# First mixer of a two-block model in an order that the kernel lays down itself, with fixed tile places, and the key search's row scale moved from VectorE to ScalarE

## The chip, the core and the metric

The kernel is one program on one core of a Trainium2 chip. The metric is device microseconds of one execution, from start to end; a run is compared by the median of its executions. The engines that matter here are TensorE (PE, matmuls), VectorE (DVE), ScalarE (ACT), GpSimd (POOL) and the DMA queue that SyncE (SP) issues. Each engine takes its instructions in the order in which they stand in its own queue; semaphores order the engines among each other.

## The reference, cut to what matters

The input is 512 tokens of 1024 values. The change lies in the first mixer and in the first step of the layer behind it:

```
h  = rmsnorm(x);  p = h @ w_in                    # 1024 -> 20 column blocks of 128
p_rw = p + mu0*(prev-p) + mu1*(next-p)             # token shift, first 16 blocks
r,k,v,wd,ad,gd = split(p_rw);  g = sigmoid(gd) @ g_up
for d in (forward, backward):                      # 8 heads of 64
    decay = exp(-exp(-softplus(-(w0+tanh(wd)@w_up))-0.5)); a = sigmoid(a0+ad@a_up)
    o += wkv7_scan(r, decay, k*(1+(a-1)*k_a), v, kk, a, reverse = d)   # delta-rule state, 64x64 a head
    bonus += sum(r*kd*r_k)*v
y_rwkv = (groupnorm(o) + bonus) * g;  y_pool = multiscale_pool(p[:, last 512])
x1 = x + concat(y_rwkv, y_pool) @ w_out
# next layer
h2 = rmsnorm(x1);  q = h2 @ wq                     # 16 column blocks f of 128
s  = q_f . keys_f   (128 scores a token and f);  top_k(s, 16)
```

Everything is float32. Behind the key search come routing, two passes over a 16,384 row expert table, and a second block; none of that is rewritten.

## The kernel before, in words

Data lie transposed: 128 features on the partitions, 512 tokens along the row. A matmul against a large weight is done in three passes in fp32r, with both operands split in a high and a low part (`Lin.mm`, L141; `Lin.mm_rows`, L154, which takes two column blocks at a time): `lo*whi`, `hi*wlo`, `hi*whi`. A weight block comes in by DMA (`wraw`), ACT copies its high part (L70, `whi`), DVE or POOL subtracts for the low part (L71, `wlo`). Blocks of w_in are loaded in four parts of two k steps, and a block is asked for one ahead (`lin.load(order[n + 1])` in `w_in`).

The first mixer runs from 0 to about 478 us. It computes w_in's 20 column blocks f (480 matmuls) and, in four quarters i of two heads, these steps: `front(i)` (L347; head norm L330 and L343, decay and gate projections L371, sigmoids, a scan, exponentials, then the in-chunk products `kb,za` and `rd,kb` L318), `invert(i)` (L435; inverts 32x32 triangles: a chain of small DVE operations L469/L470, transposes L473/L475, 32x32 matmuls L488 to L517), `solve(i)` (L523), `chain(i)` (L565; seven steps of the state over chunks, PE to DVE L585 and back) and `back(i)` (L589; group norm, bonus, gate). Gate (L231) and pooling (L257) lie in between. Then `project` multiplies with w_out in three pieces: `project(4, 4)` for the pooled half, `project(0, 3)` for quarters 0 to 2 and `project(3, 1)` for quarter 3; each of its blocks f ends with DVE adding the PSUM bank to `xt` (L655), and in the last piece also with the split `hu`, `lu` for the next layer (L77, L78) and the sum of squares `sums` (L86, L87). `inv_rms` and `spread` (L102, L108) turn that into `rb2`, the root of each token, along the row on all partitions.

The first `w_in` blocks, `front(0)` to `chain(0)`, the other `w_in` blocks with `back(0)`, and quarters 1 to 3 are written out in this order (L612 to L683). Which instruction stands where in each engine's queue is decided by the framework's scheduler, which may hoist over that order. Tiles come from rotating pools, two banks of PSUM each for `ppb`, `ppf` and `ppw`, one each for `ppi` and `ppz`.

The key search (L786 to L824) takes f = 0 and 1 by `mm_rows` and the other 14 by `mm`; each PSUM block goes through DVE (`q = ps * rb2`, L814), four matmuls with the keys (L817), one ACT copy of 128x512 (L820) and `top16` on DVE for four groups of tokens (L779 to L784). For f under 8, `normed(f)` makes `h` on DVE (L797), and PE turns a part of it (L800).

Of the kernel before, what the change touches and what calls it, by code (L numbers as in the profile page):

```python
# [46 lines left out]

@with_exitstack
def tile_two_blocks(ctx: ExitStack, tc: tile.TileContext, a: dict, out: bass.AP):
    nc = tc.nc  # L50
    V, S, G, PE = nc.vector, nc.scalar, nc.gpsimd, nc.tensor
# [4 lines left out]

    const = mk(ctx, "const", 1)
    ident = const.tile([128, 128], F32, name="ident")
    vec = const.tile([128, NVEC], F32, name="vec")
    nc.sync.dma_start(vec, a["vec"])  # L60
# [12 lines left out]
    nb = mk(ctx, "nb", 2)  # L73
# [40 lines left out]
    class Lin:  # L114
# [47 lines left out]
    cx1 = ctx.enter_context(ExitStack())  # L162
    with ExitStack() as c1:
        pooled_d = dram.tile([4, 128, T], F32, name="pooled_d")
        gate_d = dram.tile([4, 128, T], F32, name="gate_d")
        ppb = mk(c1, "ppb", 2, PSUM)
        ppf = mk(c1, "ppf", 2, PSUM)
        ppi = mk(c1, "ppi", 1, PSUM)
        ppz = mk(c1, "ppz", 1, PSUM)
        ppw = mk(c1, "ppw", 2, PSUM)  # L170
        lw = mk(c1, "lw", 1)
# [93 lines left out]
        def w_in(n):  # L265
# [6 lines left out]
            if 1 <= n and n + 1 < len(order):  # L272
                lin.load(order[n + 1])
# [1207 lines left out]
```

## Time and profile before

| | us |
|---|---|
| median of 3 runs (lowest to highest) | 2991.76 (2989.59 to 2994.38) |
| profiled execution | 2990.21 |
| its span | 2988.4 |
| PE busy in the span | 2858.1 (96%) |
| DVE busy | 1895.3 (63%) |
| ACT busy | 1198.6 (40%) |
| POOL busy | 937.7 (31%) |

PE is busy nearly all the time, but busy is not the same as quick: the profile also gives the clock that was granted to PE, as a share of full speed, and it falls in the first mixer. For a stretch of the span, idle time plus (1 - granted clock) times busy time is what PE lost against running through at full clock.

### The profile page before, as it was taken

To read this page: it belongs to the slowest core of one execution; us is meant where nothing else is said; L and a number is where in the kernel's file an instruction comes from. 1 tells how busy PE (TensorE), PEld (TensorE's weight loads), DVE (VectorE), ACT (ScalarE), POOL (GpSimd) and SP (SyncE) were. 2 spreads that over 40 slices of the span, in tenths; PEclk is the share of its full clock that TensorE was granted. 3 is DMA by queue.
4 is the path that set the end of the run, shared out by engine and by line. 5 is a ranking of instruction groups with operands and counts; after the bars stand their busy time and mean duration, and the time that the engine had idled before them with its cause. 6 is when DMAs were issued, how large, how long until landed. Compare 5 with 4: busy or idle time off the path is not lost.

```text
span 2988.4 us, 45289 instructions
## 1 busy us (share of the span) xinstructions
PE 2858.1 (96%) x17713; PEld 2394.9 (80%) x17713; DVE 1895.3 (63%) x3317; ACT 1198.6 (40%) x2073; POOL 937.7 (31%) x595
## 2 busy tenths in 40 slices
PE   8997899999999999999999999999999999999998
PEld 6666777799999877799999977888876667888887
DVE  7567637899997477777777786332269644633311
ACT  6344334247778333333333334332234343433322
POOL 1012134212331212143434414444431333244443
PEclk9898989999999999999999999999999999999999
DMA  3141123267886899999999952233331122322332
GB/s 117 58 133 31 41 63 133 71 196 262 293 304 246 297 312 315 317 313 312 316 318 326 320 174 72 98 99 95 96 104 50 59 62 62 113 89 94 99 93 77
DMA packets 201749, 495.46 MB, mean 166 GB/s; under 512 B 17616, under 2 KB 95312, under 8 KB 199616
## 3 DMA queue, kind: packets, MB, share of 16 engines
q1 hardware_dynamic: 164672, 358.34, 36.5%
q0 software_dynamic: 36864, 134.23, 12.9%
q8 instruction: 139, 2.28, 0.3%
q14 instruction: 74, 0.61, 0.1%
HBM read 446.53 MB, written 45.22 MB: 165 GB/s over the span
## 4 chain that ended last, share of the span: by engine, by line
PE 62%; DVE 19%; issue 7%; ACT 4%; DMA 3%; POOL 2%; SPq 0%; ACTq 0%; DVEq 0%; POOLq 0%
PE ps L141 32%; PE pss L736 12%; PE pv L1053 8%; DVE vl L987 2%; ACT vh L981 2%; DVE row L761 2%; PE ps L318 2%; PE pg L925 2%; POOL wlo L71 2%; DMA gate<-gates_d 1%; DVE o L918 1%; DVE ul L71 1%; DVE st L992 1%; DVE acc L766 1%; PE ps L154 1%
## 5 line engine op out<-in xcount | busy, mean ns | idle before, releaser
L71 POOL TENSOR_TENSOR wlo<-wraw,whi 128x1024 fp32r<-128x1024 f32 (+4 forms) x232 | 504.3, 2177 | 760.9 <-ACT whi L70 758.7
L70 ACT ACTIVATE whi<-wraw 128x1024 fp32r<-128x1024 f32 (+4 forms) x320 | 262.0, 822 | 691.6 <-PE ps L141 439.9
L755 POOL DMA_INDIRECT row<-peer_u,idx x128 | 163.3, 1275 | 494.1 <-DVE row L761 359.0
L141 PE MATMUL ps<-lo,whi 128*128 128x512 f32 x1112 | 295.4, 397 | 1.5 <-DVE pad L218 1.4
L141 PE MATMUL ps<-hi,whi 128*128 128x512 f32 x1112 | 295.8, 395 | 0.0
L141 PE MATMUL ps<-hi,wlo 128*128 128x512 f32 x1112 | 294.2, 395 | 1.0 <-POOL wlo L71 0.8
L141 PEld LDWEIGHTS ps<-hi,wlo 128*128 128x128 f32 x1112 | 207.8, 189 | 50.9 <-issue 6.5
L141 PEld LDWEIGHTS ps<-lo,whi 128*128 128x128 f32 x1112 | 207.4, 189 | 51.4 <-issue 7.3
L755 POOL DMA_INDIRECT row<-peer_v,idx x128 | 168.9, 1320 | 253.7 <-DVE acc L766 216.8
L1053 PE MATMUL pv<-vl,gh 128*128 128x512 f32 x768 | 241.9, 396 | 6.9 <-DVE vl L987 3.9
L141 PEld LDWEIGHTS ps<-hi,whi 128*128 128x128 f32 x1112 | 207.6, 188 | 47.1 <-issue 5.1
L1053 PE MATMUL pv<-vh,gh 128*128 128x512 f32 x768 | 237.6, 391 | 0.0
L1053 PE MATMUL pv<-vh,gl 128*128 128x512 f32 x768 | 236.9, 390 | 0.0
L70 ACT ACTIVATE gh<-st 128x384 fp32r<-128x384 f32 x128 | 67.2, 525 | 409.7 <-DVE st L992 294.3
L736 PE MATMUL pss<-lo,uh 128*128 128x384 f32 x1024 | 207.8, 344 | 5.4 <-ACT st L740 5.4
L736 PE MATMUL pss<-hi,ul 128*128 128x384 f32 x1024 | 201.7, 337 | 4.0 <-DVE ul L71 4.0
L736 PE MATMUL pss<-hi,uh 128*128 128x384 f32 x1024 | 200.4, 336 | 0.0
L987 DVE TENSOR_TENSOR vl<-vraw,vh 128x1024 fp32r<-128x1024 f32 x128 | 161.4, 1261 | 49.9 <-ACT vh L981 48.8
L736 PEld LDWEIGHTS pss<-lo,uh 128*128 128x128 f32 x1024 | 181.2, 191 | 10.9 <-ACT st L740 6.1
L736 PEld LDWEIGHTS pss<-hi,ul 128*128 128x128 f32 x1024 | 180.8, 189 | 4.6 <-DVE ul L71 4.6
L1053 PEld LDWEIGHTS pv<-vl,gh 128*128 128x128 f32 x768 | 140.6, 188 | 52.1 <-DVE vl L987 25.2
L736 PEld LDWEIGHTS pss<-hi,uh 128*128 128x128 f32 x1024 | 180.5, 189 | 0.0
(439 smaller groups left out, 5209.6 us busy)
## 6 DMA issues: line engine op xcount, KB each, us to landing
uraw<-peer_ut SPq DMA_DIRECT2D x128, 512.0 KB
vraw<-peer_v SPq DMA_DIRECT2D x128, 512.0 KB
wraw<-ffn_w_in SPq DMA_DIRECT2D x88, 512.0 KB
gates_d<-stg SPq DMA_DIRECT2D x12, 2048.0 KB
gate<-gates_d SPq DMA_DIRECT2D x32, 768.0 KB
wraw<-w_in SPq DMA_DIRECT2D x40, 512.0 KB
wraw<-ffn_w_out SPq DMA_DIRECT2D x32, 512.0 KB
st_d<-st SPq DMA_DIRECT2D x58, 192.0 KB
```

Source lines behind the costliest of these rows:

```text
L70: S.activation(hi, src, AF.Copy)
L71: eng.tensor_sub(lo, src, hi)
L141: PE.matmul(ps, w_[:, k, :m], x_[:, k0 + k, :], start=n == 0, stop=n == last)
L154: PE.matmul(ps, w_[:, k, :], x_[:, k0 + k, :], start=k0 + k + n == 0, stop=k0 + k == self.kd - 1 and n == 2)
L318: PE.matmul(ps[j:j + 64], w_[j:j + 64], x_[j:j + 64], start=start, stop=stop, tile_position=(j, j))
L736: PE.matmul(ps, w_[:, k, :], x_[:, k, :ND], start=n == 0, stop=n == 23)
L755: G.indirect_dma_start(out=r, out_offset=None, in_=tab, in_offset=bass.IndirectOffsetOnAxis(ap=idx[:, i:i + 1], axis=0))
L761: V.scalar_tensor_tensor(r, r, 1.0, htok, op0=ALU.mult, op1=ALU.mult, accum_out=act[:, s:s + 1])
L925: PE.matmul(pg[:, i, :], oo[1][:, e + i, :], oo[0][:, e + i, :], start=True, stop=True)
L981: S.activation(vh, vld[b], AF.Copy)
L987: V.tensor_sub(vl, raw, vh)
L1053: PE.matmul(pv[t * 2 + e], l_[:, ts_], r_[:, e * 512:(e + 1) * 512], start=b == 0 and q == 0, stop=b == 127 and q == 2)
```

## The change

In the first mixer the engines are wrapped (`Engine`). While the plan is open, a call isn't issued; it is noted as a node with what it reads and writes (`Plan.note`; up to 1.4 us of like PE calls on one PSUM bank make one node). `Plan.flush` gives each node a rank, the longest estimated way to the end, and places the nodes by list scheduling: the engine that can start first takes, of its ready nodes, the one of highest rank. The nodes are then issued in the order of their planned starts, under `tc.manual_schedule()`, which leaves that order as it is. There are three flushes: behind w_in and quarter 0, behind `back(2)`, and at the mixer's end. `Turns` gives each tag fixed tiles taken in turn. A weight part is noted where it is used (`Lin.take`), and the plan decides how early it is loaded. In the second part `chain` and `back` write to `ppw` banks. All noted instructions carry the line of the issuing call, L222. The key search scales the scores by `rs2` in four ACT copies in place of scaling `q` on DVE.

```diff
+class Plan:
+    STEP, SLACK, UNIT = 0.05, 0.3, 1.4
...
+    def cost(self, e, op, args, kw):
+        size = max(_free(args[0]), _free(args[1]) if op in ("max", "tensor_reduce") else 0)
+        if e == "PE":
...
+            t = max((4 * n / 2400 if full else n / 2400) + 0.013 * (1 + full), 0.05)
+            t = t / 4 if k == 32 and m == 32 else t / 2 if m == 64 else t
+            return max(t, 0.014), t + 0.2, (k == 128, m >= 128, full)
...
+        for v in reversed(nodes):
+            v["rank"] = v["until"] + max((nodes[j]["rank"] for j in v["after"]), default=0.0) + self.STEP
...
+            i = max((i for i in waiting[e] if nodes[i]["ready"] <= t + self.SLACK),
+                    key=lambda i: (nodes[i]["rank"] - 2.0 * turn(nodes[i]) - 4.0 * max(0.0, nodes[i]["ready"] - t), -i))
...
+        order.sort(key=lambda i: nodes[i]["start"])
+        with self.tc.manual_schedule():
+            for i in order:
+                for real, op, args, kw in nodes[i]["calls"]:
+                    getattr(real, op)(*args, **kw)
...
+class Turns:
...
+        n = self.n[tag] = self.n.get(tag, -1) + 1
+        key = f"{tag}_{n % (bufs or self.bufs)}"
...
-    nb = mk(ctx, "nb", 2)
+    nb = turns(ctx, "nb", 3)
...
+        def take(self, f, p):
+            if (f, p) not in self.ready:
+                self.load_part(f, p)
+            return self.ready.pop((f, p))
...
-            if 1 <= n and n + 1 < len(order):
-                lin.load(order[n + 1])
...
-            po = qd["po"] = psb()
+            po = qd["po"] = psb(outs)
...
         for n in range(8, 20):
             w_in(n)
+        plan.flush()
         cw.close()
-        open_slots(1, "right")
-        open_slots(2, "right")
+        open_slots(1, "right", plan.free["PE"])
+        open_slots(2, "right", plan.free["PE"])
+        plan.begin()
+        outs = ppw
         front(1)
...
         back(2)
+        outs = ppb
+        plan.flush()
         slots[2][1].close()
         slots[1][1].close()
+        plan.begin()
...
-        rb2 = spread(psb(ppi), inv_rms(total(psb(ppi), sums), 1e-5), xu)
-        nc.sync.dma_start(x1_d, xt)
+        rs2 = inv_rms(total(psb(ppi), sums), 1e-5)
+        rb2 = spread(psb(ppi), rs2, xu)
+        SP.dma_start(x1_d, xt)
+        plan.flush()
...
-                    V.tensor_mul(q, ps, rb2)
+                    S.activation(q, ps, AF.Copy)
...
-                    S.activation(s_.rearrange("p t n -> p (t n)"), ps, AF.Copy)
+                    for t in range(4):
+                        S.activation(s_[:, t, :], ps[:, t * 128:(t + 1) * 128], AF.Copy, scale=rs2[:, t:t + 1])
```

Three places show how instructions move. The first is PE's queue where w_in ends and quarter 1 begins. Before, the last matmuls of w_in (L141) are followed at once by quarter 1's `kb,za`; all that quarter 1 needs ahead of it stands further up, among w_in. Then comes the head of quarter 2 (L330, L343, L371) and quarter 1's inversion (L488).

```order
L141 MATMUL ps<-lo,whi 128x512 x2
L141 MATMUL ps<-hi,wlo 128x512 x2
L141 MATMUL ps<-hi,whi 128x512 x2
L318 MATMUL ps<-kb,za 64x128 x16
L318 MATMUL ps<-cst,v 64x64 x16
L318 MATMUL ps<-cst,vf 64x64 x16
L318 MATMUL ps<-cst,za 64x64 x16
L318 MATMUL ps<-rd,kb 64x128 x32
```

The same place of the change; here `rd,th` belongs to `chain(0)`, `y,cst` and the first `cst,vf` to `back(0)`, `cst,e` and `ident,rsTrue` to quarter 1's head norm.

```order
L222 MATMUL ps_117<-rd_0_174,th_184 64x64 x2
L222 MATMUL ps_123<-lo_105,whi_128 128x512 x2
L222 MATMUL ps_123<-hi_104,wlo_129 128x512 x2
L222 MATMUL ps_123<-hi_104,whi_128 128x512 x2
L222 MATMUL ps_120<-y_197,cst_90 128x512
L222 MATMUL ps_156<-sg_159,rbo_153 128x512
L222 MATMUL ps_117<-cst_90,vf_186 128x2 x4
L222 MATMUL ps_158<-cst_90,e_0_154 128x2 x4
L222 MATMUL ps_158<-lora_91,wup_152 128x512
L222 MATMUL ps_120<-ident,rsFalse_198 64x128 x8
L222 MATMUL ps_156<-ident,rsTrue_1901 64x128 x8
L222 MATMUL ps_156<-lora_91,wup_152 128x512
```

Quarter 0 now lasts until w_in's last six matmuls, and quarter 1's head stands behind them; four more rows on (two `lora,wup` and the two transposes of v) comes its `kb,za`.

The second place is DVE's queue at the end of the mixer, `project(3, 1)`. Before:

```order
L78 SCALAR_TENSOR_TENSOR lu<-xt,vec,hu 128x512
L655 TENSOR_TENSOR xt<-xt,ps 128x512
L78 SCALAR_TENSOR_TENSOR lu<-xt,vec,hu 128x512
L87 TENSOR_TENSOR sums<-sums,sq 128x512
L78 SCALAR_TENSOR_TENSOR lu<-xt,vec,hu 128x512
L655 TENSOR_TENSOR xt<-xt,ps 128x512
L87 TENSOR_TENSOR sums<-sums,sq 128x512
L655 TENSOR_TENSOR xt<-xt,ps 128x512
```

and in the change, from the eighth and last addition to `xt` on:

```order
L222 TENSOR_TENSOR xt_3937<-xt_3937,ps_123 128x512
L222 TENSOR_TENSOR sums_3958<-sums_3958,pd_3943 128x512
L222 SCALAR_TENSOR_TENSOR lu_3957<-xt_3937,vec,hu_3956 128x512
L222 TENSOR_TENSOR sums_3958<-sums_3958,pd_3943 128x512
L222 SCALAR_TENSOR_TENSOR lu_3957<-xt_3937,vec,hu_3956 128x512
L222 TENSOR_SCALAR ms_3959<-ps_185 128x4
L222 SCALAR_TENSOR_TENSOR lu_3957<-xt_3937,vec,hu_3956 128x512
L222 RECIPROCAL rs_3960<-ms_3959 128x4
L222 SCALAR_TENSOR_TENSOR lu_3957<-xt_3937,vec,hu_3956 128x512 x5
L1018 SCALAR_TENSOR_TENSOR h<-xt_3937,vec,rb_3961 128x512 x4
L1000 MAX vals<-s 128x8 x2
```

All eight additions to `xt` and six of the seven sums now stand ahead of the first `lu`, and four `h` stand ahead of the first `top16`.

The third place is PE's queue there: before, `project(3, 1)` (L141) and the key search's `mm_rows` (L154) alternate,

```order
L154 MATMUL ps<-hu,wlo 128x512
L141 MATMUL ps<-pl,whi 128x512
L141 MATMUL ps<-ph,wlo 128x512
L141 MATMUL ps<-ph,whi 128x512
L154 MATMUL ps<-hu,whi 128x512
L154 MATMUL ps<-lu,whi 128x512
L154 MATMUL ps<-hu,wlo 128x512
L154 MATMUL ps<-hu,whi 128x512
```

and in the change `mm_rows` (L368) begins when `project(3, 1)` has ended:

```order
L222 MATMUL ps_123<-pl_3942,whi_3951 128x512
L222 MATMUL ps_123<-ph_3941,wlo_3952 128x512
L222 MATMUL ps_123<-ph_3941,whi_3951 128x512
L368 MATMUL ps<-lu_3957,whi 128x512
L222 MATMUL ps_185<-ones,sums_3958 128x1 x4
L368 MATMUL ps<-hu_3956,wlo 128x512
L368 MATMUL ps<-hu_3956,whi 128x512
L368 MATMUL ps<-lu_3957,whi 128x512
```

The sum of squares over the partitions (`ones,sums`) stands behind the first of the 48 `mm_rows` matmuls, where before it stood ahead of the last three.

## Rows read from the trace of the kernel before

**Rows 1.** Windows: length, busy us (PE, PEld, DVE, ACT, POOL), PEclk, DMA share, GB/s.

```profile
0.00:23.00 23.00, 15.32 (x57) 11.23 (x58) 14.39 (x35) 15.99 (x30) 2.93 (x10) 1.00 0.71 231
23.00:224.00 201.00, 182.24 (x1738) 136.42 (x1740) 129.63 (x238) 87.85 (x157) 19.41 (x23) 0.93 0.29 88
80.00:100.00 20.00, 16.78 (x279) 7.29 (x278) 14.31 (x38) 5.19 (x9) 1.18 (x2) 0.74 0.21 69
224.00:421.00 197.00, 167.61 (x3672) 141.87 (x3669) 123.95 (x242) 78.35 (x128) 37.64 (x38) 0.90 0.14 44
245.00:279.00 34.00, 24.20 (x609) 19.16 (x610) 26.38 (x54) 18.66 (x27) 8.62 (x9) 0.75 0.11 27
421.00:478.00 57.00, 52.14 (x219) 39.19 (x218) 25.77 (x38) 22.00 (x42) 28.71 (x26) 0.94 0.31 97
478.00:600.00 122.00, 109.37 (x537) 87.59 (x536) 104.22 (x531) 37.30 (x56) 42.23 (x21) 1.00 0.28 95
```

**Rows 2.** Waits of PE, 224 to 478: us, times, longest.

```profile
PE ps L488 <- DVE dt L473: 9.9, 3, 7.3
PE ps L141 <- POOL pl L71: 3.5, 3, 2.1
PE ps L318 <- DVE th L585: 1.9, 2, 1.2
```

**Rows 3.** Timeline of PE, quarter 0's head: start, busy us, instructions, [idle before].

```profile
41.86 0.95 PE L330 MATMUL ps<-cst,sq 128*128 128x2 f32 x8
...
58.99 1.96 PE L318 MATMUL ps<-kb,za 64*64 64x128 f32 x32 [1.46 <-DVE za L392]
```

**Rows 4.** Timeline of PE, quarter 2's head and quarter 1's inversion.

```profile
244.53 0.95 PE L330 MATMUL ps<-cst,sq 128*128 128x2 f32 x8
...
260.72 1.93 PE L488 MATMUL ps<-dt,lo 32*32 32x32 f32 x128 [7.33 <-DVE dt L473]
```

**Rows 5.** Timeline of PE, mixer's end and three steps of the key search.

```profile
465.11 0.39 PE L141 MATMUL ps<-pl,whi 128*128 128x512 f32 x1
...
484.83 1.13 PE L108 MATMUL ps<-ident,rs 128*128 128x128 f32 x8
...
539.37 1.13 PE L817 MATMUL ps<-keys,q 128*128 128x128 f32 x8 [0.52 <-DVE q L814]
540.34 0.27 PE L800 MATMUL pt<-ident,h 128*128 128x128 f32 x1
...
546.28 1.13 PE L817 MATMUL ps<-keys,q 128*128 128x128 f32 x8 [0.52 <-DVE q L814]
...
596.21 1.13 PE L817 MATMUL ps<-keys,q 128*128 128x128 f32 x8 [0.61 <-DVE q L814]
```

**Rows 6.** Timeline of DVE, first `top16` and the first instruction behind the last.

```profile
494.87 0.49 DVE L779 MAX8 vals<-s 128x8 f32<-128x128 f32 x2
...
603.13 0.29 DVE L833 CAST idf<-ids 128x256 f32<-128x256 uint32 x1
```

**Rows 7.** Groups of DVE, 462 to 495: busy us, mean ns, idle before.

```profile
L655 DVE TENSOR_TENSOR xt<-xt,ps 128x512 f32<-128x512 f32 x10 | 6.8, 681 | 4.3 <-PE ps L141 4.3
L78 DVE SCALAR_TENSOR_TENSOR lu<-xt,vec,hu 128x512 fp32r<-128x512 f32 x8 | 6.2, 775 | 1.1 <-ACT hu L77 1.1
L87 DVE TENSOR_TENSOR sums<-sums,sq 128x512 f32<-128x512 f32 x7 | 5.1, 732 | 0.0
```

**Rows 8.** Groups of all engines, 478 to 603.

```profile
L797 DVE SCALAR_TENSOR_TENSOR h<-xt,vec,rb 128x512 f32<-128x512 f32 x8 | 12.5, 1586 | 0.0
...
L814 DVE TENSOR_TENSOR q<-ps,rb 128x512 f32<-128x512 f32 x16 | 10.8, 678 | 3.5 <-ACT rb L111 1.9 <-PE ps L817 1.6
L820 ACT ACTIVATE s<-ps 128x512 f32<-128x512 f32 x16 | 9.5, 596 | 26.8 <-PE ps L817 25.8 <-DVE mr L782 1.0
...
L801 ACT ACTIVATE htok<-pt 128x128 f32<-128x128 f32 x8 | 2.2, 270 | 1.2 <-PE pt L800 1.2
```

**Rows 9.** Groups of ACT, 600 to 1000: a 128x128 copy with a pointer scale.

```profile
L921 ACT ACTIVATE o<-o,gtr 128x128 f32<-128x128 f32 x384 | 126.0, 393 | 42.4 <-DVE o L918 42.3
```

More of the change, by code (lines that the diff above doesn't have):

```diff
@@ new lines, in _free, with __init__, tile @@
+def _free(ap):
+    n = 1
+    for d in ap.shape[1:]:
+        n *= d
+    return n
+class Turns:
+    def __init__(self, plan, pool, bufs, born=0.0):
+        self.plan, self.pool, self.bufs, self.born, self.n, self.places = plan, pool, bufs, born, {}, {}
+    def tile(self, shape, dtype, tag=None, name=None, bufs=None):
+        tag, size = tag or name, 1
+        for d in shape[1:]:
+            size *= d
+        n = self.n[tag] = self.n.get(tag, -1) + 1
+        key = f"{tag}_{n % (bufs or self.bufs)}"
+        if key not in self.places:
+            t = self.places[key] = self.pool.tile([128, size], dtype, tag=key, name=key, bufs=1)
+            self.plan.born[t.tensor.name] = self.born
+        t = self.places[key][:shape[0], :size]
+        if len(shape) == 3:
+            t = t.rearrange("p (a b) -> p a b", b=shape[2])
+        elif len(shape) == 4:
+            t = t.rearrange("p (a b c) -> p a b c", b=shape[2], c=shape[3])
+        return t
@@ L55, in mk, with turns @@
         return c.enter_context(tc.tile_pool(name=name, bufs=bufs, side=side, reuse_waits="tile", **kw))
+    def turns(c, name, bufs, space=None, side=None, born=0.0):
+        return Turns(plan, mk(c, name, bufs, space, side), bufs, born)
     const = mk(ctx, "const", 1)
@@ L297, in w_in @@
                 pooling(f - 16, ps)
[L302 to L303 removed]
+        yb = turns(c1, "yb", 3)
+        tp = turns(c1, "tp2", 1)
         yt = {}
@@ L637, in tile_two_blocks @@
         back(2)
+        outs = ppb
+        plan.flush()
         slots[2][1].close()
         slots[1][1].close()
-        xp = mk(cx1, "xp3", 1, side="right")
+        plan.begin()
+        xp = turns(cx1, "xp3", 1, side="right")
         xt = xp.tile([128, KD, T], F32, name="xt")
         for k in range(0, KD, 2):
-            nc.sync.dma_start(xt[:, k:k + 2, :], xdram[:, k:k + 2, :])
-        wp = mk(c1, "wp3", 1)
+            SP.dma_start(xt[:, k:k + 2, :], xdram[:, k:k + 2, :])
+        wp = turns(c1, "wp3", 1)
         def split2(k, src, xh, xl, eng):
@@ L676, in tile_two_blocks @@
                 project(0, 3, ph, pl)
-        xu = mk(cx1, "xu", 1, side="right")
+        xu = turns(cx1, "xu", 1, side="right")
         hu = xu.tile([128, KD, T], F32R, name="hu")
```

262 lines of the change are left out of this document (198 added, 64 removed).

## The prediction

> **What bounds the kernel now.** I read the page first, then the windows of the first mixer, then PE's waits, then the timelines at three seams. The reader should see in the windows that PE is the engine to count: wherever DVE is not nearly full, the time of a stretch is PE's work, plus its idle time, plus what the lowered clock costs. I count the loss of a stretch as idle + (1 - granted clock) x busy. From 23 to 224 us, where w_in and quarter 0 run, that is 18.8 + 0.07 x 182.2 = 31.5 us; from 224 to 421, quarters 1 to 3, 29.4 + 0.10 x 167.6 = 46.2 us; from 421 to 478, w_out, 4.9 + 0.06 x 52.1 = 8.0 us [rows 1]. So at most some 86 of the mixer's 478 us can be won by order alone, as no work is taken away there. The clock follows the idle time: the worst windows, 80 to 100 and 245 to 279, have 0.74 and 0.75, a mean between the two levels of 2.4 and 1.2 GHz, in the one with 3.2 and in the other with 9.8 us of idle PE [rows 1]. In the key search, 478 to 600, the clock is 1.00, PE idles 12.6 us and DVE 17.8 [rows 1], and in the steady part each f costs a stall of PE on DVE's `q` [rows 5].
>
> **Part 1, w_in and quarter 0.** Before, quarter 0's steps are done early with few w_in matmuls between them, and a long run of w_in follows. The new order puts six w_in matmuls (at times 12 or more) between nearly all of quarter 0's dependent pieces: 31 runs of w_in in place of 23, the last of them behind `chain(0)`. A DVE answer that PE now waits for is covered by 1.4 us of w_in. I let two thirds of the 31.5 us come back, -20; the ends are 0 (each wait stays) and -31. Against it, quarter 1's head used to stand among w_in and now follows its last matmuls. In quarter 0 it is 17.1 us from L330 to `kb,za` [rows 3]; quarter 2's head keeps PE some 260.72 - 244.53 - 7.33 = 8.9 us at work [rows 4], so a bubble of up to 8 us is opened. `back(0)` stands in it, and the square for the head norm is made earlier than before; I take +5, between 0 and +8. In the lead, gate weights, pool counts, `wup` and the identity of the inversion (1.28 MB by their shapes) are now issued ahead of the last four blocks of x: 5.5 us at the 231 GB/s of the first 23 us, in which PE idles 7.7 [rows 1]; I take +2, between 0 and +5.5. Part 1: -13.
>
> **Part 2, quarters 1 to 3.** There is no w_in left here, before or after; only the quarters can fill each other. PE's largest wait, L488 on `dt`, 9.9 us in three [rows 2], has its 7.33 us piece behind the head of quarter 2 [rows 4], and in the new order quarter 2's head stands ahead of L488 in just the same way. So that piece shrinks only as far as DVE is ordered better: its inversion operations are a long chain and get a high rank, where before they share DVE with `front(2)`. `chain(1)` is now mixed with `front(3)`'s projections and `invert(2)`, `chain(2)` with `invert(3)`. The outputs in `ppw` banks free the two that `solve` turns. I take a fifth of 46.2, -9; the ends are +9 (a fifth more, if the fixed order fits badly) and -30 (two thirds, as in part 1).
>
> **Part 3, w_out.** The three waits on POOL's `pl`, 3.5 us [rows 2], lie between `project(4, 4)` and `project(0, 3)`. In the new order all 96 matmuls of `project(4, 4)` come first, and then four of `chain(3)`'s steps without anything between them. During these POOL gets done, so the 3.5 go; the four steps wait for DVE instead, at 0.3 to 1.2 us each (the longest such wait has 1.2 [rows 2]). I take +1.5 for them: -2, between -3.5 and +1.3.
>
> **Part 4, hand-over and key search.** I count from T, the first matmul of `project(3, 1)`, before at 465.11; `mm_rows` ends about T + 19.7 [rows 5], the first `top16` is at T + 29.8 and routing begins at T + 138.0 [rows 6]. After: DVE does eight additions at 0.681 and seven sums at 0.732 with the first `lu`, 0.775, among their end: 11.3 us [rows 7], so that `lu` is there at about T + 12.2. The 24 matmuls of the projection cover only some 5.4 of that; then PE waits. The 48 matmuls of `mm_rows` follow. One f costs 546.28 - 539.37 = 6.91 us, of which 0.52 are the stall and 0.97 the keys' matmuls [rows 5], so 24 matmuls take 5.42 and 48 take 10.8; with the column sum and the spread among them `mm_rows` ends at T + 24, 4.3 us later than before. From there it is better: `q` needs no `rb2` and no DVE, `h` for four blocks is already made in the gap, and DVE has lost 10.8 us [rows 8]. ACT's copy of `q` takes about 0.6, as its 128x512 copy of scores does [rows 8]; keys of f = 1 begin at T + 25.8; 14 more at 6.39 (no stall) bring the last to T + 115.3; from the last keys to routing it is 603.13 - 596.21 = 6.9 us [rows 5, 6]: T + 122.2. That is -15.8. But PE has only four or five matmuls, 0.9 to 1.1 us, between an f's end and its keys, and in these ACT must get its turn and copy for 0.6. ACT's four scaled copies cost between 4 x 270 and 4 x 393 ns [rows 8, 9] in place of 596 ns, 0.5 to 1.0 more each f; ACT is busy 37.3 of 122 us [rows 1], so they fit, though one may stand ahead of a `q`. I add 0.3 for each of 14 f, +4.2, and 1.6 for the clock after the gap at T: -10. The ends are -16 (no stall) and -2 (1.0 each). DVE doesn't set this: of its 104.2 us [rows 1] 93.4 are left without `q`, 5.8 an f, and four of the eight `h` of 1.59 us [rows 8] are made ahead of it.
>
> The Trainium skill, "ScalarE: Activation LUTs", section "Rules for kernel authors", advises VectorE and not ScalarE for multiplications, which speaks against this edit. Its section "What ACT_TABLE_LOAD costs" gives 186 ns + 0.833 ns an element and about 93 ns for a pointer operand; worked out by that, an estimate, four scaled copies are 1.5 us and the one before 0.61. The trace agrees with 393 and 596 ns. By that rule the key search would be dearer by 0.9 us of ACT for each f and nothing for PE, as long as PE bounds it.
>
> **Sum.** -13 - 9 - 2 - 10 = -34. The profiled execution took 2990.2, its span and 1.8 us around it, 1.6 under the median shown; 2990.2 - 34 = 2956. Behind the key search nothing is rewritten, and I leave it as it is.
>
> **Rivals.** *A, only the seams give.* Quarters 1 to 3 are bound by their own chain through PE and DVE, whatever the order: DVE is busy 26.4 of 34 us in 245 to 279 [rows 1], and the head of quarter 2 still stands ahead of L488. Part 1 wins half (-16) with the full bubble of 8 and the lead's 2, part 2 gives 0, and the key search the -4 of a stall near 0.9: -6 + 0 - 2 - 4 = -12, 2978. For it speaks that no filler is added there; against it that 16.8 of the 46 us are clock, which any better packing wins back.
>
> *B, nearly all comes back.* The quarters overlap as planned and the clock stays up: -26 in part 1, -24 in part 2, -2, -13: -65, 2925. For it: the estimates of cost behind the plan need to be right only in order, not in size. Against it: the same head and L488.
>
> *C, slower: the fixed order waits at each return.* PE takes its queue in order, and 31 times it now goes from w_in to a small dependent piece whose place was set by estimates. If DVE is late there, w_in behind it waits too, which before was often hoisted past. If each return costs 0.9 us, about what a single wait on such a piece shows (1.9 in two [rows 2]), 28 us of idle time stand in place of 18.8; with the clock's 12.8 as before and the 7 of bubble and lead, part 1 is 28 + 12.8 + 7 - 31.5 = +16. Part 2 ends at its +9 by the same mechanism: +16 + 9 - 2 - 10 = +13, 3003. The point from which it decides is about 0.7 us a return (part 1 +10, part 2 +9, in all +7); the forecast's 11.5 us of loss left in part 1 is 0.37. Against it: DVE is busy only 64% of 23 to 224 [rows 1], so that lateness doesn't pile up.
>
> The Trainium skill, "TensorE: Matmul & The Clock Gate", section "Why this matters for your kernels", warns of idle gaps between bursts of matmuls, behind which the array falls to the lower clock. The trace agrees (0.74 and 0.75). By it the two new gaps, at quarter 1's head and at T, would cost more than their idle time; rival C is the case where such gaps come at many places.
>
> *D, the mixer is as before.* The order changes but its critical chain doesn't, and only part 4 counts, reduced by its later `mm_rows`: -5, 2985.
>
> **How the numbers follow.** A measurement of this kernel tells about 0.2% or 6 us from no change. Forecast, 2938 to 2974: 0.50. A, up to 2984: 0.17. B, below 2938: 0.13. D and small remains, 2984 to 2996: 0.09. C, above 2996: 0.11. So faster 0.80, same 0.09, slower 0.11. The time is that of the likeliest, 2956; its own range is 2938 to 2974. The range for 8 in 10 takes in A and D and most of B: 2921 to 2995.
>
> **What would show it.** Part 1: loss by the same count from PE's 23rd us to the end of w_in near 11 us, and w_in's last matmul some 14 us ahead of quarter 1's `kb,za` (8.9 of work, 5 of idle time). Part 2: clock over 0.93, a wait for `dt` of 4 to 7 us still there. Part 3: no wait on POOL's `pl`. Part 4: PE idle about 6 us before the first `mm_rows` matmul, a period of 6.4 to 6.8 us for each f, routing at T + 124 to T + 130. It is wrong if quarter 1's head costs over 10 us, if w_in's returns show waits over 0.5 us in the mean, or if the period for each f stays at 6.9.

## The result, and the profile after

The changed kernel takes 2956.78 us (median of 4 runs, 2948.96 to 2967.07) against 2993.07 (4 runs) before: a ratio of 0.9882, 95% interval 0.985 to 0.9914. The same program in a second series had 2958.21 (5 runs), ratio 0.9896, 0.9876 to 0.9916. The forecast was 2956. Its four terms did not come out alike, as the profiled execution shows (2948.96 us, the fastest of the four; span 2946.0, 42.4 us less than before):

| stretch | before, us | after, us | difference | second sample after | forecast |
|---|---|---|---|---|---|
| start to quarter 1's `kb,za` | 223.64 | 214.64 | -9.0 | -5.9 | -13 |
| from there to T, the first matmul of `project(3, 1)` | 241.47 | 216.66 | -24.8 | -24.0 | -11 |
| T to routing | 138.02 | 136.48 | -1.5 | -1.9 | -10 |
| routing to the end | 2385.31 | 2378.19 | -7.1 | -1.8 | 0 |

The page, granted clock of PE in 40 slices, before and after (the second profile of the changed kernel, below as after_again, has an 8 in slices 4 and 7):

```profile
PEclk9898989999999999999999999999999999999999
PEclk9999999999999999999999999999999999999999
```

The windows of the mixer and the key search, after (length, busy us of PE, PEld, DVE, ACT, POOL, granted clock, DMA share, GB/s):

```profile
23.00:198.00 175.00, 168.63 (x1689) 126.15 (x1689) 115.01 (x221) 76.69 (x145) 12.00 (x17) 1.00 0.31 98
198.00:262.00 64.00, 45.05 (x766) 34.93 (x764) 52.89 (x93) 29.75 (x41) 15.24 (x17) 0.89 0.10 30
262.00:385.00 123.00, 112.94 (x2875) 98.55 (x2871) 81.83 (x165) 60.06 (x102) 23.84 (x23) 0.97 0.19 59
385.00:431.00 46.00, 45.06 (x277) 35.99 (x271) 14.94 (x27) 12.39 (x24) 20.64 (x21) 1.00 0.18 52
431.00:449.00 18.00, 8.06 (x24) 4.72 (x24) 14.81 (x18) 12.57 (x23) 10.80 (x9) 0.84 0.60 190
449.00:466.00 17.00, 16.92 (x64) 13.76 (x64) 7.60 (x13) 4.50 (x9) 4.24 (x3) 0.77 0.47 186
466.00:570.00 104.00, 103.94 (x526) 86.49 (x526) 90.07 (x526) 49.45 (x113) 38.19 (x18) 1.00 0.27 84
```

By idle + (1 - clock) x busy, w_in and quarter 0 lose 6.4 us where they lost 31.5 [rows 1]. The loss that is left sits in three places: 198 to 262 (18.95 + 0.11 x 45.05 = 23.9 us), 431 to 449 (11.2) and, in clock alone, 449 to 466 (4.0). From 262 to 431, `chain`, `solve` and `invert` of the quarters with `project(4, 4)` and `project(0, 3)`, it is 14.4 us.

The count promised more than it paid. From 23 us to quarter 1's `kb,za`, before and after:

```profile
23.00:223.64 200.64, 181.88 (x1732) 136.06 (x1732) 129.38 (x237) 87.85 (x157) 19.21 (x22) 0.93 0.29 88
23.00:214.64 191.64, 180.00 (x1812) 133.36 (x1812) 127.87 (x241) 87.69 (x160) 18.03 (x24) 1.00 0.30 95
```

The loss falls from 31.5 to 11.6 us, 19.9 less; with 3.3 us more idle time in the first 23 us that would be -16.6, where `kb,za` came 9.0 earlier. Idle time makes 3.8 of the 9.0 (7.1 less, 3.3 more). PE's busy time fell by only 1.9 us at a clock that rose from 0.93 to 1.00, where the count has 12.7 for the clock. The stretch holds 80 matmuls more, 16 that the first 23 us did not do and 64 (`cst,v`, `cst,vf`) that stood behind `kb,za` before: some 6 us, an estimate from 0.23 us for each of the 16 and 2.0 for the 64. The rest, some 5 us, (1 - clock) x busy counts too much; why is open.

The first place in PE's timeline (start, busy us, instructions, idle before and its releaser): w_in's last matmuls, quarter 1's head norm and projections, its `kb,za`, then quarter 1's inversion and quarter 2's `kb,za`.

```profile
197.19 0.63 PE L222 MATMUL ps<-hi,whi 128*128 128x512 f32 x2
...
200.28 1.03 PE L222 MATMUL ps<-cst,e 128*128 128x2 f32 x8
202.05 1.13 PE L222 MATMUL ps<-lora,wup 128*128 128x512 f32 x2 [0.74 <-ACT rsTrue L222]
...
206.28 3.03 PE L222 MATMUL ps<-lora,wup 128*128 128x512 f32 x6 [1.21 <-DVE nkk L222]
...
214.64 3.56 PE L222 MATMUL ps<-kb,za 64*64 64x128 f32 x32 [3.32 <-DVE kb L222]
...
249.97 1.29 PE L222 MATMUL ps<-ld,lo 32*32 32x32 f32 x128 [3.05 <-DVE ld L222]
253.77 3.68 PE L222 MATMUL ps<-kb,za 64*64 64x128 f32 x32 [2.51 <-DVE kb L222]
```

From the start of w_in's last row to `kb,za` it is 17.5 us, from the head norm 14.4, where quarter 0 took 17.1 before [rows 3]; little is left to cover it. From this `kb,za` to the next quarter's it is 39.1 us. Before it was 39.5:

```profile
223.64 1.96 PE L318 MATMUL ps<-kb,za 64*64 64x128 f32 x32
...
263.10 2.39 PE L318 MATMUL ps<-kb,za 64*64 64x128 f32 x18 [0.44 <-DVE za L392]
```

So no time was won there, and nearly all of the second stretch's 24.8 us lie behind quarter 2's `kb,za`. From there to T, before and after:

```profile
263.10:465.11 202.01, 181.75 (x3362) 152.42 (x3363) 105.38 (x199) 75.78 (x131) 53.57 (x48) 0.90 0.19 60
253.77:431.30 177.53, 166.23 (x3363) 142.19 (x3363) 103.88 (x201) 75.13 (x130) 44.78 (x44) 0.97 0.18 54
```

The matmuls are as many, 24.5 us are gone, and the loss by the count falls from 38.4 to 16.3 us.

The second place, PE at the hand-over to the key search:

```profile
431.30 0.47 PE L222 MATMUL ps<-pl,whi 128*128 128x512 f32 x1 [0.39 <-DVE xt L222]
...
439.29 0.50 PE L222 MATMUL ps<-ph,wlo 128*128 128x512 f32 x1 [2.48 <-POOL wlo L222]
...
449.08 0.77 PE L368 MATMUL ps<-lu,whi 128*128 128x512 f32 x1 [6.41 <-DVE lu L222]
449.72 1.87 PE L222 MATMUL ps<-ones,sums 128*128 128x1 f32 x8
...
453.30 1.91 PE L222 MATMUL ps<-ident,rs 128*128 128x128 f32 x8
...
465.62 0.40 PE L368 MATMUL ps<-hu,whi 128*128 128x512 f32 x1
```

PE waits 2.48 us for a low part on POOL and 6.41 for `lu`, and the first of the 48 matmuls of `mm_rows` take 0.63 us where the last take 0.40. They end 34.7 us behind T, before 19.7 [rows 5].

The same time on DVE, then on POOL and in SP's queue:

```profile
443.09 2.42 DVE L222 TENSOR_TENSOR sums<-sums,pd 128x512 f32<-128x512 f32 x1 [0.79 <-ACT pd L222]
445.44 0.68 DVE L222 TENSOR_TENSOR xt<-xt,ps 128x512 f32<-128x512 f32 x1
446.21 2.07 DVE L222 TENSOR_TENSOR sums<-sums,pd 128x512 f32<-128x512 f32 x1
448.20 0.74 DVE L222 SCALAR_TENSOR_TENSOR lu<-xt,vec,hu 128x512 fp32r<-128x512 f32 x1
```

```profile
436.02 2.35 POOL L282 TENSOR_TENSOR wlo<-wraw,whi 128x1024 fp32r<-128x1024 f32 x1 [0.97 <-ACT whi L281]
...
442.61 5.11 POOL L282 TENSOR_TENSOR wlo<-wraw,whi 128x1024 fp32r<-128x1024 f32 x2 [1.98 <-ACT whi L281]
```

```profile
416.59 14.64 SPq L222 DMA_DIRECT2D wraw<-w_out  x7
431.28 0.42 SPq L341 DMA_DIRECT2D wraw<-wq  x1
```

Two of the sums take 2.4 and 2.1 us beside POOL's low parts of wq (L282), where others have 0.69. The low part of w_out for which PE waits 2.48 us stands in POOL's queue behind the one of wq at 436.02. The first load of wq is issued at T; before, it was issued 18.2 us ahead of T:

```profile
446.87 0.43 SPq L127 DMA_DIRECT2D wraw<-wq  x1
```

The key search itself, three of its steps, and the first `top16` and the start of routing on DVE:

```profile
547.52 1.15 PE L1038 MATMUL ps<-keys,q 128*128 128x128 f32 x8
554.10 1.14 PE L1038 MATMUL ps<-keys,q 128*128 128x128 f32 x8
560.64 1.16 PE L1038 MATMUL ps<-keys,q 128*128 128x128 f32 x8
```

```profile
469.85 0.47 DVE L1000 MAX8 vals<-s 128x8 f32<-128x128 f32 x2
...
567.78 0.29 DVE L1055 CAST idf<-ids 128x256 f32<-128x256 uint32 x1
```

An f takes 6.54 to 6.58 us here, and the stall on `q` [rows 5] is gone.

### The profile page after: what moved, and what is told of

Its sections match the earlier page's. It is cut to its first block, busy times and chain, and to the rows that moved or that the text cites. A ratio compares the mean times of both kernels' runs of the same rounds, so it can differ in the third digit from the quotient of the medians.

```text
span 2946.0 us, 45351 instructions
## 1 busy us (share of the span) xinstructions
PE 2835.0 (96%) x17713; PEld 2378.8 (81%) x17713; DVE 1882.9 (64%) x3301; ACT 1215.2 (41%) x2137; POOL 936.2 (32%) x595
## 4 chain that ended last, share of the span: by engine, by line
PE 68%; DVE 16%; issue 7%; ACT 4%; DMA 2%; POOL 2%; ACTq 0%; SPq 0%; DVEq 0%; POOLq 0%
PE ps L358 32%; PE pss L957 13%; PE ps L222 9%; PE pv L1275 8%; DVE vl L1209 3%; ACT vh L1203 2%; DVE row L982 2%; PE pg L1147 2%; POOL wlo L282 1%; DVE o L1140 1%; DVE st L1214 1%; DVE ul L282 1%; DMA gate<-gates_d 1%; DVE acc L987 1%; PE ps L368 1%
## 5 line engine op out<-in xcount | busy, mean ns | idle before, releaser
L282 POOL TENSOR_TENSOR wlo<-wraw,whi 128x1024 fp32r<-128x1024 f32 (+2 forms) x208 | 481.8, 2317 | 712.1 <-ACT whi L281 709.8
L281 ACT ACTIVATE whi<-wraw 128x1024 fp32r<-128x1024 f32 (+2 forms) x216 | 218.3, 1012 | 570.2 <-PE ps L358 363.8
L358 PE MATMUL ps<-hi,whi 128*128 128x512 f32 x968 | 249.4, 394 | 0.0
L358 PE MATMUL ps<-hi,wlo 128*128 128x512 f32 x968 | 248.5, 395 | 0.7 <-POOL wlo L282 0.7
L358 PE MATMUL ps<-lo,whi 128*128 128x512 f32 x968 | 246.0, 393 | 0.1
L358 PEld LDWEIGHTS ps<-hi,wlo 128*128 128x128 f32 x968 | 180.3, 189 | 43.9 <-issue 6.1
L358 PEld LDWEIGHTS ps<-lo,whi 128*128 128x128 f32 x968 | 179.9, 188 | 41.1 <-issue 3.6
L358 PEld LDWEIGHTS ps<-hi,whi 128*128 128x128 f32 x968 | 180.1, 188 | 40.3 <-issue 4.0
```

The costliest lines, as they stand in the source:

```text
L281: S.activation(hi, src, AF.Copy)
L282: eng.tensor_sub(lo, src, hi)
L358: PE.matmul(ps, w_[:, k, :m], x_[:, k0 + k, :], start=n == 0, stop=n == last)
```

## Experiments

Each ratio is against the kernel before, run on the same chip in the same series. There are five series, in which the kernel before had medians of 2988.30 to 2994.58 us, so runs of different series are compared by their ratios. Landmarks come from one profile each: `kb,za` is the first such matmul of quarter 1, T the first matmul of `project(3, 1)`.

| run | median us | ratio, 95% interval | `kb,za` | T | `kb,za` to T | T to first `top16` | T to routing |
|---|---|---|---|---|---|---|---|
| before | 2993.07 | 1 | 223.6 | 465.1 | 241.5 | 29.8 | 138.0 |
| after | 2956.78 | 0.9882, 0.985 to 0.9914 | 214.6 | 431.3 | 216.7 | 38.6 | 136.5 |
| after_again | 2958.21 | 0.9896, 0.9876 to 0.9916 | 217.7 | 435.2 | 217.5 | 38.2 | 136.2 |
| key_only | 2975.43 | 0.9951, 0.9932 to 0.997 | 225.9 | 464.3 | 238.4 | 30.2 | 129.0 |
| no_key | 2968.24 | 0.9929, 0.991 to 0.9948 | 217.6 | 438.2 | 220.6 | 37.8 | 149.3 |
| lu_rank | 2961.50 | 0.9907, 0.9884 to 0.9929 | 220.4 | 436.4 | 215.9 | 40.9 | 139.8 |
| tail_out | 2954.64 | 0.9880, 0.9856 to 0.9904 | 218.9 | 433.1 | 214.2 | 35.2 | 134.8 |
| plan1_only | 2974.65 | 0.9939, 0.9919 to 0.9958 | 220.2 | 466.1 | 245.8 | 29.0 | 125.1 |
| plan23_only | 2963.99 | 0.9904, 0.9882 to 0.9927 | 227.6 | 444.8 | 217.2 | 38.8 | 136.7 |
| outs_ppb | 2964.36 | 0.9907, 0.9887 to 0.9928 | 218.8 | 445.0 | 226.2 | 38.7 | 136.6 |
| w_out_out | 2952.46 | 0.9872, 0.9848 to 0.9896 | 217.0 | 440.5 | 223.5 | 29.0 | 126.3 |
| head_in | 2950.55 | 0.9860, 0.9837 to 0.9884 | 216.1 | 431.9 | 215.9 | 38.2 | 136.1 |
| both | 2949.42 | 0.9857, 0.9835 to 0.9880 | 213.0 | 436.1 | 223.1 | 29.0 | 127.6 |
| both_x | 2950.04 | 0.9854, 0.9833 to 0.9874 | 216.0 | 438.8 | 222.7 | 29.0 | 127.5 |

**after_again**, the changed kernel once more.

> The changed kernel once more, unaltered, as a second sample of the same program, because its four runs lay between 2948.96 and 2967.07 us at granted clocks between 0.987 and 0.979. Theory (the spread is the granted clock in stretches that the change doesn't touch): the mixer's landmarks come again within 2 us of the first profile (last w_in matmul 197, first matmul of the last w_out piece 431, routing 568) and any difference in the total lies behind routing. Rival (the fixed order itself is unsteady): the landmarks up to 431 move by 5 us or more between the two profiles. Median expected 2957.

Neither holds alone. The two profiles differ by 8.9 us of span: 3.1 at `kb,za`, 3.9 at T, 3.6 at routing, and 5.3 behind it. So landmarks of one program may differ by about 4 us, and no less is read from a single one below. For `kb,za` even that is short: the plan's first part is the same in eight of the runs in the table (after, after_again, no_key, lu_rank, tail_out, plan1_only, outs_ppb, w_out_out), and there it lies between 214.6 and 220.4, in the mean at 218.2. The 214.6 of the first profile is the earliest of the eight; against the 223.6 and 225.9 of before and key_only the mean is 5 to 8 us earlier.

**key_only**, on the kernel before; it also keeps `rs2` and gives the pool `nb` that holds it three buffers, as in the change.

```diff
-                    V.tensor_mul(q, ps, rb2)
+                    S.activation(q, ps, AF.Copy)
...
-                    S.activation(s_.rearrange("p t n -> p (t n)"), ps, AF.Copy)
+                    for t in range(4):
+                        S.activation(s_[:, t, :], ps[:, t * 128:(t + 1) * 128], AF.Copy, scale=rs2[:, t:t + 1])
```

> The kernel before with only the key search's edit (copy of q on ScalarE, four scaled copies). Theory (the edit is worth its 10 us wherever the hand-over from the mixer is not worse): first matmul of the last w_out piece stays at 465, the period of an f falls from 6.91 to about 6.5, routing begins some 127 us behind that matmul in place of 138.0: 2982. Rival (PE bounds this stretch and the edit moves only work between engines that wait): the period stays within 0.1 of 6.9 and the time within 3 us of the kernel before, 2990.

The theory holds: 129.0 us from T to routing, 9.1 fewer, at a period of 6.52 to 6.58 in the second half; the ratio excludes 1. The first half is slower: two steps take 11.0 and 8.2 us, in one of them PE waits 3.1 us for an `h` that here is not made ahead of the key search.

**no_key**, the changed kernel with these lines turned back.

```diff
-                    S.activation(q, ps, AF.Copy)
+                    V.tensor_mul(q, ps, rb2)
...
-                    for t in range(4):
-                        S.activation(s_[:, t, :], ps[:, t * 128:(t + 1) * 128], AF.Copy, scale=rs2[:, t:t + 1])
+                    S.activation(s_.rearrange("p t n -> p (t n)"), ps, AF.Copy)
```

> The changed kernel with the key search's edit undone (VectorE scales q by rb2, one copy of the scores). Theory (the laid-down order gives about 34 us, and the edit in the changed kernel some 7 more that the late hand-over eats up): from the first matmul of the last w_out piece to routing about 145 us in place of 136.5, total 2965. Rival (the edit does nothing here, the hand-over alone decides): 137 us and 2957.

149.3 us from T to routing, 12.8 more, periods of 7.22 and stalls on `q` again; in all 10 us more than after_again in the same series, so the theory holds by size. The two edits add: 14.6 us or so for one, 21 for the other, 31 to 36 together. The laid-down order made the stretch from T longer, by 11.3 us with the old key search (149.3 against 138.0) and by 7.3 with the new (136.3 against 129.0).

**lu_rank**, a rank for what the plan doesn't see.

```diff
+            out = max((self.later.get(p[0], 0.0) for p in v["writes"]), default=0.0)
-            v["rank"] = v["until"] + max((nodes[j]["rank"] for j in v["after"]), default=0.0) + self.STEP
+            v["rank"] = v["until"] + max([out] + [nodes[j]["rank"] for j in v["after"]]) + self.STEP
...
+        for t in (hu, lu):
+            plan.later[t.tensor.name] = 11.0
```

> The changed kernel, but the plan gives the nodes that write hu and lu a rank of 11 us more, about the 48 matmuls of the key search that read them and that the plan doesn't see. Theory (lu came last because nothing in the plan hangs on it): the lu splits stand among the additions, PE's wait of 6.4 us before the first of these matmuls and the half clock behind it go, the 48 matmuls end some 22 to 25 us behind the first matmul of the last w_out piece in place of 34.6, routing is 126 to 129 us behind it in place of 136.5: 2948. Rival (the wait was for work that must be done anyway, and the sum of squares and rb2, now later, hold up the scaled copies): no gain over 2 us, 2955 to 2960.

No gain: the rival. PE shows why (the first and the last `mm_rows` matmul, the sum behind them, the spread), and DVE the cause:

```profile
446.45 0.54 PE L369 MATMUL ps<-lu,whi 128*128 128x512 f32 x1
...
460.16 0.40 PE L369 MATMUL ps<-hu,whi 128*128 128x512 f32 x1
465.67 1.87 PE L223 MATMUL ps<-ones,sums 128*128 128x1 f32 x8 [5.11 <-DVE sums L223]
...
468.40 1.92 PE L223 MATMUL ps<-ident,rs 128*128 128x128 f32 x8
```

```profile
447.26 9.01 DVE L223 SCALAR_TENSOR_TENSOR lu<-xt,vec,hu 128x512 fp32r<-128x512 f32 x7
456.19 0.68 DVE L223 TENSOR_TENSOR sums<-sums,pd 128x512 f32<-128x512 f32 x1
457.56 0.69 DVE L223 TENSOR_TENSOR sums<-sums,pd 128x512 f32<-128x512 f32 x1 [0.70 <-ACT pd L223]
```

The mechanism named was there: with a rank, `lu` comes early and `mm_rows` begins without its 6.4 us wait and ends 24 us behind T. But now the sums come last, one in 1.4 us as they share one `pd` tile with ACT, and PE, whose queue holds the sum ahead of the next f, waits 5.11 us for them. The wait moved from one side to the other.

**tail_out**, the plan ended ahead of `project(3, 1)`.

```diff
+        plan.flush()
         project(3, 1, ph[:, 3:], pl[:, 3:], done=sums)
...
         SP.dma_start(x1_d, xt)
-        plan.flush()
```

> The changed kernel with the last flush of the plan ahead of the last w_out piece, so that this piece, the sum of squares and rb2 are ordered by the framework's scheduler together with the key search, as before. Theory (the plan doesn't see the key search behind it, so it puts lu last, and with a higher rank for lu it put the sums last; only one schedule over both sides gets both early): from the first matmul of the last w_out piece to routing 129 us, as where the key search's edit was made on the kernel before (128.97), in place of 136.2 to 136.5; in all 2950. Rival (the 7 us are due to what goes on at POOL and ScalarE by then, the early loads of wq, whoever orders): 135 to 137 us and 2957.

134.8 us: 1.5 less than after, by landmarks not to be told from none; the rival. The order of `lu` and sums at DVE is mixed again and yet the time is not back, so that order isn't the main cause. A `lu` and a sum beside POOL's low parts of wq still take 2.3 and 2.9 us there:

```profile
441.19 2.28 DVE L289 SCALAR_TENSOR_TENSOR lu<-xt,vec,hu 128x512 fp32r<-128x512 f32 x1
443.39 2.88 DVE L298 TENSOR_TENSOR sums<-sums,pd 128x512 f32<-128x512 f32 x1
```

```profile
440.52 2.40 POOL L282 TENSOR_TENSOR wlo<-wraw,whi 128x1024 fp32r<-128x1024 f32 x1 [0.41 <-DMA wraw<-wq]
443.22 2.50 POOL L282 TENSOR_TENSOR wlo<-wraw,whi 128x1024 fp32r<-128x1024 f32 x1 [0.30 <-ACT whi L281]
```

These rows show more than a slower rate. Each of the two ends 0.55 us behind the subtraction that was running when it began (443.47 and 442.92, 446.27 and 445.72): it waits for the end of that instruction. All 14 profiles show the same from 425 to 500 us. Every `sums`, `lu` or `h` that began while POOL was in a subtraction, with at least 0.17 us of it to go, ended 0.54 to 0.56 us behind it, and with 0.03 us to go it took its usual 0.69.

**w_out_out**, the plan ended one piece earlier.

```diff
         project(4, 4, ph, pl)
+        plan.flush()
...
         SP.dma_start(x1_d, xt)
-        plan.flush()
```

> The changed kernel with the plan's last flush right behind project(4, 4): both later pieces of w_out, the sum of squares and rb2 are ordered by the framework's scheduler. On SP's queue the loads of wq then stand again among those of w_out, the first of them eight loads earlier than where the plan ends behind project(3, 1). Theory (what was lost at the hand-over is the late load of wq: its low parts, 2.4 us each on GpSimd, fall into the last w_out piece, and VectorE's sums and lu beside them take 2.3 to 2.9 us in place of 0.7): the splits of wq lie ahead of the last piece, VectorE's slow operations there go, routing begins 125 to 130 us behind its first matmul in place of 134.8 (flush one piece later) and 136.3 (flush at the end), total 2947. Rival (these 7 us are the price of a shorter mixer, as wq's tiles come free no earlier): 133 to 136 us and 2955.

126.3 us: the theory. SP issues the first load of wq at 422.49, again 18 us ahead of T (440.51), and POOL's three subtractions on wq's first blocks all lie ahead of T. In the changed kernel they lie behind it (POOL's groups, first of the changed kernel from 431.3 to 466, then of this one from 420 to 440.5):

```profile
L282 POOL TENSOR_TENSOR wlo<-wraw,whi 128x1024 fp32r<-128x1024 f32 x3 | 7.5, 2504 | 2.9 <-ACT whi L281 2.9
L282 POOL TENSOR_TENSOR wlo<-wraw,whi 128x1024 fp32r<-128x1024 f32 x3 | 7.2, 2394 | 1.1 <-ACT whi L281 1.1
```

DVE's groups behind T (busy us, mean ns, idle before), of the changed kernel from 431 to 466, then of this one from 440 to 466:

```profile
L222 DVE TENSOR_TENSOR sums<-sums,pd 128x512 f32<-128x512 f32 x7 | 9.1, 1300 | 2.2 <-ACT pd L222 1.9
L222 DVE TENSOR_TENSOR xt<-xt,ps 128x512 f32<-128x512 f32 x10 | 6.7, 681 | 1.0 <-PE ps L222 1.0
```

```profile
L874 DVE TENSOR_TENSOR xt<-xt,ps 128x512 f32<-128x512 f32 x9 | 6.1, 679 | 3.1 <-PE ps L358 3.1
L298 DVE TENSOR_TENSOR sums<-sums,pd 128x512 f32<-128x512 f32 x7 | 5.1, 730 | 0.0
```

A sum, both of whose inputs lie in SBUF, falls from 1300 to 730 ns, the 732 of before [rows 7]; an addition that reads PSUM stays at 680. Of the 10 us won behind T, 6 are paid ahead of it: `project(0, 3)` is no longer in the plan, waits on POOL are back there (2.8 us on `pl`, 1.6 on low parts), and `kb,za` to T grows from 217 to 223.5. In all it is 4 to 6 us under the changed kernel's medians, with intervals that overlap; at 2952.46 the total is nearer the rival's 2955 than the theory's 2947. No run moved wq's loads alone: what the framework's scheduler does with `project(0, 3)` came with them.

**plan1_only** and **plan23_only**, the plan used for w_in and quarter 0 alone (no second and third part), or only behind them.

```diff
-        plan.begin()
         outs = ppw
         front(1)
...
-        plan.flush()
         slots[2][1].close()
         slots[1][1].close()
-        plan.begin()
...
-        plan.flush()
```

```diff
     cx1 = ctx.enter_context(ExitStack())
-    plan.begin()
...
         for n in range(8, 20):
             w_in(n)
-        plan.flush()
```

> The plan is used for w_in and quarter 0 alone; quarters 1 to 3, w_out and the key search's hand-over are ordered by the framework's scheduler (with the fixed places and the output banks of the change). Theory (part 1 gave about 9 us at quarter 1's first kb,za, parts 2 and 3 about 22): kb,za of quarter 1 at 215 to 219, first matmul of the last w_out piece at 453 to 458, routing 129 us behind it: 2971. Rival (the gain of parts 2 and 3 comes from the fixed places and the output banks, not from the order): last piece at 435, 2952.

> The plan is used for quarters 1 to 3 and w_out; w_in and quarter 0 are ordered by the framework's scheduler. Theory: kb,za of quarter 1 at 223 to 226 (as before), from there to the first matmul of the last w_out piece 216 to 221 us in place of before's 238 to 241.5, routing 136 us behind: 2966. Rival (the gain behind w_in needs the early end of w_in's loads and of quarter 0): 230 us or more in that stretch, 2978.

Part 1 alone gave nothing that can be told: 2974.65 beside key_only's 2975.43 (other series; ratios 0.9939 and 0.9951, intervals overlapping). Its `kb,za` is at 220.2, which was expected within 215 to 219, and T at 466.1, where 453 to 458 was expected: what was won at `kb,za` was used up in quarters 1 to 3. The rival, that places and banks do it, falls too. The plan behind w_in gives `kb,za` to T in 217.2 us whatever came before, as the theory of plan23_only had it. With both, the median is some 6 us under plan23_only's (intervals overlapping), and T 10 to 14 us earlier.

**outs_ppb**, the banks as before.

```diff
-        outs = ppw
```

> The changed kernel, but the outputs of chain and back go to the ppb banks in quarters 1 and 2 as before. Theory (the two ppb banks are turned by solve while a chain holds one of them, so that solve of the next quarter can't run beside it): the stretch from quarter 1's kb,za to the first matmul of the last w_out piece grows from 216 to 221 by 5 to 10 us: 2965. Rival (order alone): within 2 us, 2957.

226.2 us from `kb,za` to T, 9 more, and 2964.36 in all (its interval overlaps with the changed kernel's): the theory. So of the 24 us of that stretch the two more banks gave about 9, but only under the plan's order (in plan1_only, which has them too, the stretch is 245.8).

**head_in** and **both**. In head_in, `front` is split: `head(1)` is noted in the plan's first part.

```diff
+        def head(i):
+            qd = Q[i] = {}
...
+            return rT, kT, vT, rbo, nkk, sga
...
+        heads[1] = head(1)
+        for t in heads[1][4:5] + tuple(heads[1][5]):
+            plan.later[t.tensor.name] = 20.0
         plan.flush()
```

> The changed kernel with quarter 1's head (head norm, decay and gate projections, sigmoids) noted in the plan's first part, with a rank of 20 us more for its outputs, so that it can stand among w_in's matmuls. Theory (the bubble at the seam is due to the flush between w_in and quarter 1): from w_in's last matmul to quarter 1's kb,za 7 to 10 us in place of 17 to 19, kb,za at 207 to 212, everything behind it earlier by as much: 2951. Rival (VectorE, which has scan, products and kb to make behind the head, sets that time): kb,za earlier by 3 us at most, 2955 to 2958.

> The two edits before together: quarter 1's head in the plan's first part, and the plan ended behind project(4, 4). Theory: the gains add, as they lie in stretches 200 us apart: 2941. Rival (what comes earlier at the first seam is lost again in quarters 1 to 3, as where the plan was used for part 1 alone): 2948, as with the second edit alone.

In head_in `kb,za` follows w_in's last matmul (206.00, later by the head's work) after 10.1 us in place of 17.5; but it is at 216.1, no earlier than can be told from the 214.6 to 220.4 of the same place without the edit: the rival at the landmark, though the median fell to 2950.55 (intervals overlapping). Both together, 2949.42, are 1.1 us under head_in alone and 3 under w_out_out: the gains don't add, and this time `kb,za` to T is 223 again. It is the fastest median here, 7 to 9 us under the changed kernel's; its interval's end, 0.988, overlaps with 0.985 and 0.9876, where theirs begin.

**both_x**, also eight tiles for x.

```diff
-                xk = xp.tile([128, T], F32, tag="xk", name="xk", bufs=4)
+                xk = xp.tile([128, T], F32, tag="xk", name="xk", bufs=8)
```

> The two edits together and eight tiles for the blocks of x in place of four, so that the plan issues all of x ahead of gate weights, pool counts and the inversion's identity. Theory (in the lead the last four blocks of x come behind 1.28 MB of other loads, which PE pays with a wait of 2.6 to 3.7 us near 18 us): that wait goes, w_in's last matmul and quarter 1's kb,za come 3 to 4 us earlier than with both edits (204.6 and 213.0 there), total 2946. Rival (the first weights then come later by as much, or the time is lost in quarters 1 to 3 again): landmarks within 1.5 us, total 2948 to 2951.

The rival: the wait near 18 us went, three others of 1.0 to 1.7 us (`acc`, `rs`, a weight's high part) came, `kb,za` is no earlier, 2950.04.

## Why the prediction was right, and where it wasn't

The total was right within 1 us, and that is luck: parts 2 and 3 gave 13 to 14 us more than forecast, part 4 gave 8 less and part 1 4 to 7 less, and behind routing, where nothing was forecast, the two profiles are 7 and 2 us shorter than the one before.

- **Part 1** was forecast at -13 and is -9.0 and -5.9, by the mean of eight profiles -5 to -8. The mechanism held: loss of 6.4 us (11 forecast) and an idle bubble of 0.74 + 1.21 + 3.32 = 5.3 at quarter 1's head (5). `kb,za` stands 17.5 us behind w_in's last row where 14 was named, as PE has 11.4 us of work from 198 us on, not 8.9; `back(0)` is among it. Two terms were mis-sized. The larger is the clock's share of the loss, 12.7 of the 31.5 us, of which some 5 did not come. The smaller is the lead, +2 forecast and 3.3 measured: the first matmul waits until 7.93 us (before 6.97) and later ones 2.58 and 0.40 more, and PE is busy 12.0 of the first 23 us, before 15.3 [rows 1]. And plan1_only shows that what part 1 wins is worth little by itself.
- **Parts 2 and 3** were forecast at -11 and are -24.8 and -24.0. The mis-sized term is "a fifth of 46.2". That the head of quarter 2 and its L488 would not gain was right: `kb,za` to `kb,za` is 39.1 us, before 39.5, and a wait of 3.05 us on the inversion is left. But I spread the caution over the whole stretch. Behind it, where chains, solves and inversions of different quarters can fill each other, the loss fell from 202.0 - 181.8 + 0.10 x 181.8 = 38.4 us to 177.5 - 166.2 + 0.03 x 166.2 = 16.3. Nine of the 24 come with the banks (outs_ppb), which the forecast put at no price of their own.
- **Part 4** was forecast at -10 and is -1.5 and -1.9. The period was priced right (6.54 to 6.76, 6.4 to 6.8 forecast), and so was the key search as a whole: from the keys of f = 1 to routing it took 99.1 us, where the sum has 102. That key_only gives -9.1 doesn't confirm the -10, for the -10 has a hand-over that comes 4.3 us later and 1.6 of clock in it; without these the same sum gives -15.9. It counts on four `h` made in the gap, and key_only has no gap. The step that failed is "`mm_rows` ends at T + 24": it ended at T + 34.7, since `lu` was at T + 17.6 in place of 12.2 and the matmuls behind the gap ran at 0.77. The forecast counted DVE's sums at 0.732 us, the duration before; behind T, where the new order of SP's queue had pushed POOL's work on wq, they wait for the ends of POOL's subtractions and take 1300 ns in the mean, 4.0 us more for the seven. The prediction priced SP's new order only in the lead. w_out_out, where wq's loads stand earlier, gives 126.3 us, in the range 124 to 130 named for this step.
- **Part 3's** waits on `pl` are gone as forecast, and the four open steps of `chain(3)` cost 0.37 + 3 x 0.16 us.
- Of the rivals, C (a wait at each return) is refuted by the loss of 6.4 us in 23 to 198; A by the 24 us of quarters 1 to 3; D by key_only, which falls 17 to 19 us short of the changed kernel. B had parts 2 and 3 nearly right (-26), but its -26 and -13 for parts 1 and 4 did not come.

On two VectorE operations that slow beside GpSimd, the Trainium skill, "GPSIMD Engine Reference", section "1. Specifications", says that GpSimd shares its SBUF interfaces with VectorE, with contention for VectorE instructions with two SBUF inputs. The trace agrees: 2.42 and 2.07 us beside POOL's subtraction and 0.69 without for a sum with two SBUF inputs, and 0.68 throughout for an addition with one input in PSUM.

What stays open: why behind routing, where the programs are nearly alike, the profiles differ by up to 8.8 us (2378.1 in w_out_out to 2386.9 in lu_rank), why an earlier `kb,za` is sometimes lost again by T, and how much of the 10 us of w_out_out is due to wq's loads alone. None was settled by a run.

## What to carry to other kernels

A schedule laid down for one stage doesn't see who reads its results: here it put the next stage's operand last, and its loads behind its own; look at the last things it emits, on every queue, and give either the reader's work or an earlier end of the plan (w_out_out won 10 us behind the seam and paid 6 ahead of it). Don't count the whole price of a lowered clock as a gain: here some 5 of 12.7 us, by an estimate, did not come. When pricing a reordering, split the stretch at the places where the old critical order stays, and let the gain come from the rest alone. A duration is only as good as its neighbours: ask which engine will now run beside it, and whether one of its instructions has to end first.

## What the runs showed of the hardware

VectorE additions of 128x512 float32 with both inputs in SBUF took 0.67 to 0.69 us at their fastest. Where they began while GpSimd was in a subtraction, they ended 0.55 us behind its end, so that beside one of 128x1024 they took up to 2.9 us (tail_out); those with an input in PSUM stayed at 0.68. PE's granted clock, a mean of the levels 1.2 and 2.4 GHz in each stretch, fell to 0.84 in the 18 us with the waits of 2.48 and 6.41 us, in which PE was busy for 8.06, and was 0.77 in the 17 us behind it, though PE was busy in 16.92 of them.
